# Key pages laid out with features on partitions, and weights laid out tile by tile, in a two-layer decoder step

## The chip, the cores and the metric

The kernel runs on one core of a Trainium2 chip. The metric is the device time of one execution in microseconds (us). Engines are named as the profile names them: PE (TensorE, matrix products; PEld its weight loads), DVE (VectorE), ACT (ScalarE), POOL (GpSimd), and SP (SyncE, which issues most DMAs here). A "q" behind an engine's name means its sequencer, as where it issues a DMA.

## The reference

One inference step of a decoder with two layers, for a prompt of 1024 tokens and for 8 sequences of 8 sample tokens, all in float32. Layer 0 is stick-breaking attention, layer 1 an RWKV-7 recurrence; each is followed by a squared-ReLU MLP, and each of the four sub-layers has a norm with shift, scale and gate made from a conditioning vector (adaLN). What matters here is the attention of the sample tokens: each sequence has 2048 past keys and values in 16 pages of 128 tokens, and a page table says where in the pool they lie.

```python
def sb_attend(q, k, v, q_pos, k_pos, bias):
    z = einsum('bqhd,bkhd->bhqk', q, k) * (SB_HEAD_DIM ** -0.5) + bias[None, :, None, None]
    mask = k_pos[None, :] < q_pos[:, None]
    log_beta = log_sigmoid(z)
    log_1mb = where(mask, log_beta - z, 0.0)
    tail = cumsum(log_1mb, axis=3, reverse=True) - log_1mb
    a = where(mask, exp(log_beta + tail), 0.0)
    return einsum('bhqk,bkhd->bqhd', a, v)

past_k = cache_k[layer][page_table]     # 8 sequences x 16 pages x 128 tokens x 16 heads x 64
past_v = cache_v[layer][page_table]
```

The weight of a key depends on all later keys, so a sequence is worked through from its last page to its first with a carried product.

## The kernel before

Activations lie with features on partitions, in 8 tiles of 128 features, and the tokens on the free axis in two halves: A (576 columns, the 64 sample tokens among them) and B (512). A dense layer (`dense`, L354) takes one tile of 128 outputs at a time. `weight` (L340) loads the tile's weights (wst; 128 x 8 x 128, or 128 x 4 x 128 for the MLP's second half) straight from the row-major matrix, so that each descriptor moves 128 floats, 512 bytes. ACT rounds them to wh, POOL and DVE make the rest wl, and PE sums three products for each tile of inputs (dq at L364 to L366).

Behind the dense layers runs other work, as a generator: after every so many dense products one step of it is put into the program (`step`, `behind`). `background` (L1588) holds the prompt's attention of both halves, then the attention of the samples (`att_sample`, L671), then the recurrence. While the samples are attended to, half A's MLP is the dense work, and its weights are asked for by ACT's queue rather than by SP's (`self.sampling`). The written order is only a start: the scheduler puts the instructions of each engine in order by its own estimates of time, and gives the DMAs of both queues the semaphores that they wait for.

`att_sample` takes two pages a step, 64 steps in all, 8 for a sequence:

- `page_id` (L663) reads two page numbers from the table into SP's registers.
- `page_k` (L652, DMA at L657) loads a key page as it lies, tokens first, in four DMAs of a quarter of the features each: 32 partitions (key modulo 32), in each 4 runs of 256 floats. Two page buffers (`KB`) are used in turn.
- `turned` (L701, L705) transposes the page on DVE, 32 x 32 blocks at a time, into kT; this is why the features of a page were cut into tiles of (feature / 256, feature % 32). Two buffers (`KTB`).
- `scores` (L708, L714): for each of the two pages 8 products of the queries (qbd, every head in its own columns, made by `queries`, L689) with 128 columns of kT, into zs.
- `stick` (L555): sigmoid on ACT, 1 - beta on POOL, a scan and a product on DVE.
- the weights are transposed on PE (tq), copied to aTs, and multiplied with the value pages into os (L771). `page_v` (L645, DMA at L648) loads a value page in one DMA of 128 partitions with 4 KB each; five buffers (`VB`) in turn.

The scores of the next step stand ahead of this step's products, and the pages for it are asked for before that. `new_keys` handles a sequence's 8 new tokens ahead of its first step.

The vectors of features (biases, gains and the like) are loaded in rows of 128 by many small DMAs and transposed on PE in three groups (`load_params`, L147), and the conditioning vectors likewise (`load_c`, L180). The adaLN weights are read by blocks of 256 columns, 1 KB a descriptor (`ada_steps`).

Of the kernel before, what the change touches and what calls it, by code (L numbers as in the profile page):

```python
# [31 lines left out]
KTB = 2  # L32
# [32 lines left out]
def make_consts():  # L65
# [20 lines left out]
    for h in range(16):  # L86
        c[p // 8 == 4 * (h % 4) + h // 4, C_H16 + h] = 1.0
# [6 lines left out]
class Kern:  # L94
# [19 lines left out]
    def copy(self, out, in_, eng=None):  # L114
        """PSUM or SBUF to SBUF, on ScalarE and VectorE in turn."""
        if eng is None:
            eng = "a" if self.flip() else "v"
        if eng == "a":
            self.nc.scalar.copy(out, in_)  # L119
        elif eng == "v":  # L120
            self.nc.vector.tensor_copy(out, in_)  # L121
        else:
            self.nc.gpsimd.tensor_copy(out, in_)
# [23 lines left out]
    def load_params(self, groups, tmp, ps, tag):  # L147
        """Vectors of features: rows of 128 on partitions, then features on partitions."""
        nc, I = self.nc, self.I
        for group in groups:  # L150
            nrow = sum(n for _, _, n in group)
            nat = tmp.tile([128, 128], F32, tag="n", name="pnat")
            r = 0
            for name, ap, n in group:
                flat = ap if len(ap.shape) == 1 else ap.rearrange("a b -> (a b)")
                nc.sync.dma_start(nat[r:r + n, :], flat.rearrange("(a b) -> a b", b=128))
                r += n
            q = ps.tile([128, 512], F32, tag=tag, name="pps")
            self.transpose(q[:, :nrow], nat[:nrow, :])
            par = self.misc.tile([128, nrow], F32, name="par_" + group[0][0])  # L160
            self.copy(par, q[:, :nrow])
            r = 0
            for name, ap, n in group:
                self.par[name] = par[:, r:r + n]
                r += n

    def params(self):
        I = self.I
        ada = lambda s: (f"b{s}", I["ada_b_" + ("mix", "ffn")[s % 2]][s // 2], 24)
        vec = lambda n: (n, I["rw_" + n][0], 8)  # L170
        self.par = {}
        return [
            [ada(0), ("norm_mix", I["norm_mix"], 16)],
            [ada(1), ada(2), ada(3), ("norm_ffn", I["norm_ffn"], 16), ("final", I["final_norm"], 8)],
            [("mu", I["rw_mu"][0], 48)] + [vec(n) for n in ("w0", "a0", "k_k", "k_a", "r_k", "ln_g",
                                                           "ln_b")],
        ]

# [1 line left out]
    def load_c(self, tmp, ps):  # L180
        nc, I = self.nc, self.I
        c = tmp.tile([72, 128], F32, tag="n", name="c")
        nc.sync.dma_start(c[0:8], I["c_prompt"].rearrange("v (k p) -> (v k) p", p=128))
        nc.sync.dma_start(c[8:72], I["c_sample"].rearrange("v (k p) -> (v k) p", p=128))
        s = tmp.tile([72, 128], F32, tag="n", name="cs")
        nc.scalar.activation(s, c, AF.Sigmoid)
        nc.vector.tensor_mul(s, s, c)
        q = ps.tile([128, 512], F32, tag="dps", name="cps")
        self.transpose(q[:, 0:72], s)
        self.cT = self.misc.tile([128, NT, 32], F32, name="cT")  # L190
        nc.vector.memset(self.cT, 0.0)
        nc.vector.tensor_copy(self.cT[:, :, 0:9], q[:, 0:72].rearrange("p (v k) -> p k v", v=9))
# [32 lines left out]
    def ada_steps(self, s, ps, tag, blocks=range(12)):  # L225
        """mod[:, j, v]: feature tile j of shift (0-7), scale (8-15), gate (16-23); vector v.
        The scale tiles end up as norm gain * (1 + scale)."""
        nc, I = self.nc, self.I
        i, kind = s // 2, ("mix", "ffn")[s % 2]
        w = I["ada_w_" + kind][i]  # L230
# [20 lines left out]
        for n in blocks:  # L251
            q = ps.tile([128, 512], F32, tag=tag, name="adaq")
            for u in range(0, NT, kt):
                st = pool.tile([128, kt, 256], F32, tag=stage, name="adaw")
                nc.sync.dma_start(st, w[u * 128:(u + kt) * 128, n * 256:(n + 1) * 256]
                                  .rearrange("(k p) c -> p k c", p=128))
# [15 lines left out]
    def rms(self, x, pt, tmp, ps, tag, slot, rslot=None):  # L272
        """1 / sqrt(mean square + eps) of every token, on all partitions: [128, W]."""
# [26 lines left out]
    def modulate(self, s, f, x, R, pt, t):  # L300
        """t = x * R * A of feature tile f, of samples with B added; returns B of the prompt."""
# [18 lines left out]
    def norm_split(self, s, x, R, pt, pool, tmp, slot):  # L320
        """Rounded parts of (x * R) * A + B."""
# [48 lines left out]
    def residual(self, s, x, pt, tmp):  # L370
        """evac of a dense layer: x += gate * out."""
# [17 lines left out]
    def load_x(self, pt, pool, ps, early):  # L389
        """Generator; the tiles are in self.x. early: all loads first."""  # L390
# [27 lines left out]
    def to_tokens(self, m, pt, t, dst_p, dst_s, tmp, ps):  # L418
        """Feature tile m of the columns of pt; rows of tokens to DRAM."""
# [19 lines left out]
    def qkv(self, hi, lo, pt, tmp, ps):  # L439
        I, O = self.I, self.O  # L440
        w = I["sb_w_qkv"][0]
# [4 lines left out]
        self.dense_to(w[:, D:2 * D], hi, lo, pt, tmp, ps, self.s_k0,  # L446
# [5 lines left out]
        self.dense_to(w[:, 2 * D:], hi, lo, pt, tmp, ps, None, value)  # L452

# [9 lines left out]
    def load_split(self, src, pt, pool, tmp, parts):  # L463
        """Generator: rounded parts of feature tiles in DRAM."""
# [19 lines left out]
    def ffn(self, s, x, hi, lo, pt, pool, tmp, ps):  # L484
        """x += gate * (relu(h @ w_up) ** 2) @ w_down, the hidden layer 512 at a time."""
# [3 lines left out]
        for b in range(8):  # L489
# [14 lines left out]
            self.dense(wd[512 * b:512 * b + 512], range(NT), [uh[k] for k in ks],  # L504
                       [ul[k] for k in ks], pt, ps, res)

# [1 line left out]
    def att_setup(self, lp):  # L508
# [7 lines left out]
        # of the two heads of a feature tile, 64 rows each  # L516
# [9 lines left out]
    def att_stacks(self, m, pt, sp):  # L526
        """Rounded parts of q and k of the two heads of tile m, the parts of k on top of each other."""
# [27 lines left out]
    def stick(self, z, w, bias, bp, tag, carry, mask):  # L555
        """z: scores in PSUM [128, w], keys in order; returns weights a and the product of 1 - beta."""
# [17 lines left out]
    def att_prompt(self, m, pt, sp, bp, ps):  # L574
        """Generator over the query tiles (128 of a head, or 64 of both) of the two heads of tile m."""
# [69 lines left out]
    def page_v(self, sp, r):  # L645
        t = sp.tile([128, D], F32, tag="pv", name="pagev", bufs=VB)
        src = self.I["cache_v"][0].rearrange("n p h d -> n p (h d)")
        ins = self.nc.sync.dma_start(t, src[bass.ds(r, 1)].rearrange("o p f -> (o p) f"))  # L648
# [3 lines left out]
    def page_k(self, sp, r):  # L652
        """[128 (feature / 256, key % 32), key / 32, feature % 256]"""
        t = sp.tile([128, D], F32, tag="pk", name="pagek", bufs=KB)
        src = self.I["cache_k"][0].rearrange("n (i k) h d -> n k i (h d)", i=4)
        for x, a in enumerate(self.R4):
            ins = self.nc.sync.dma_start(  # L657
                t[a].rearrange("k (i f) -> k i f", i=4),
# [1143 lines left out]
```

## Time and profile before

| | us |
|---|---|
| median of 3 runs | 4046.95 (4046.1, 4046.95, 4064.11) |
| span of the profiled execution | 4045.0 |
| PE busy | 3675.1 |
| DVE busy | 2499.4 |
| ACT busy | 1491.1 |
| POOL busy | 1322.8 |

For the profiled execution the profile has its span, from the first to the last instruction; no other time of it is known, and the two closest runs lie 1.1 and 1.95 us above that span. The profile's second part cuts the span into 40 slices of 101 us and gives busy shares in tenths. A stretch of any length can be asked for in the same way, and so can the waits in it, the DMAs that its queues issued, and each instruction. In a row of a wait stand who waited, for whom, the total in us, how many times, and the longest. A matmul in float32 is two instructions in the profile.

### The profile page before, as it was taken

Reading aid. Unit: us, or ns where it says so; the run is one execution under the profiler, and the core shown is the slowest. Engines: PE = TensorE matmul, PEld = TensorE weight load, DVE = VectorE, ACT = ScalarE, POOL = GpSimd, SP = SyncE. Lnnn points to the kernel's source line nnn. Section 1 sums busy time; section 2 is a strip of 40 time slices with the busy share of each in tenths; the row PEclk is TensorE's granted clock in tenths of the full one; section 3 lists DMA queues with packets and bytes.
Section 4 is the critical chain, followed back from the end, with each engine's and each line's share of the span. In section 5 each row is a group of like instructions: output and inputs, shape, how many; then the busy total and the mean of one; then the engine's idle time right before and its main releaser. Section 6 shows DMA issues by size and latency. Waiting matters only on the chain. (4 is left out here: it accounts for less than half of the span.)

```text
span 4045.0 us, 76587 instructions
## 1 busy us (share of the span) xinstructions
PE 3675.1 (91%) x27756; PEld 2899.0 (72%) x27756; DVE 2499.4 (62%) x4907; ACT 1491.1 (37%) x3132; POOL 1322.8 (33%) x1844
## 2 busy tenths in 40 slices
PE   8989999899887888799779999999889999998998
PEld 6776667677666666577657777665688888876887
DVE  4256777886555455668775555677884666645444
ACT  4123444543121122455333444554434333433332
POOL 1135555563111111222243333433222222233442
PEclk9999999999999999799789999898899999999999
DMA  9965434125999999856645444556735444342332
GB/s 283 292 186 164 153 114 102 49 67 140 236 236 215 216 228 231 239 169 217 180 118 139 127 129 131 173 179 212 215 110 138 116 121 137 96 133 76 102 98 78
DMA packets 873728, 641.63 MB, mean 159 GB/s; under 512 B 174195, under 2 KB 793004, under 8 KB 873350
## 3 DMA queue, kind: packets, MB, share of 16 engines
q1 hardware_dynamic: 804198, 602.12, 52.8%
q10 hardware_dynamic: 69152, 34.61, 3.9%
q8 instruction: 220, 3.60, 0.4%
q14 instruction: 158, 1.29, 0.1%
HBM read 521.62 MB, written 114.92 MB: 157 GB/s over the span
## 5 line engine op out<-in xcount | busy, mean ns | idle before, releaser
L350 POOL TENSOR_TENSOR wl<-wst,wh 128x256 fp32r<-128x256 f32 (+1 forms) x512 | 641.3, 1254 | 1553.0 <-ACT wh L348 1353.0
L364 PE MATMUL dq<-hhi,wh 128*128 128x288 f32 (+1 forms) x2112 | 717.9, 341 | 29.4 <-ACT hhi L119 22.5
L348 ACT CAST wh<-wst 128x512 fp32r<-128x512 f32 (+1 forms) x512 | 424.6, 834 | 825.7 <-PE dq L365 546.2
L365 PE MATMUL dq<-hlo,wh 128*128 128x288 f32 (+1 forms) x2112 | 713.6, 338 | 7.7 <-POOL hlo L318 4.7
L366 PE MATMUL dq<-hhi,wl 128*128 128x288 f32 (+1 forms) x2112 | 715.9, 339 | 0.0
L365 PE MATMUL dq<-ul,wh 128*128 128x288 f32 (+1 forms) x1536 | 514.8, 335 | 0.0
L351 DVE TENSOR_TENSOR wl<-wst,wh 128x256 fp32r<-128x256 f32 (+1 forms) x512 | 349.5, 685 | 267.1 <-ACT wh L348 251.1
L366 PE MATMUL dq<-uh,wl 128*128 128x288 f32 (+1 forms) x1536 | 512.9, 335 | 0.0
L364 PE MATMUL dq<-uh,wh 128*128 128x288 f32 (+1 forms) x1536 | 511.2, 337 | 1.4 <-DVE x L379 0.6
L364 PEld LDWEIGHTS dq<-hhi,wh 128*128 128x128 f32 x2112 | 407.3, 193 | 72.9 <-ACT hhi L119 23.2
L365 PEld LDWEIGHTS dq<-hlo,wh 128*128 128x128 f32 x2112 | 406.9, 193 | 54.2 <-issue 14.4
L366 PEld LDWEIGHTS dq<-hhi,wl 128*128 128x128 f32 x2112 | 407.0, 193 | 49.5 <-issue 18.7
L379 DVE SCALAR_TENSOR_TENSOR x<-dq,mod,x 128x288 f32<-128x288 f32 (+1 forms) x432 | 243.2, 565 | 207.5 <-PE dq L366 204.8
L364 PEld LDWEIGHTS dq<-uh,wh 128*128 128x128 f32 x1536 | 292.2, 191 | 42.4 <-issue 14.1
L705 DVE STREAM_TRANSPOSE kT<-pagek 128x1024 f32<-128x1024 f32 x128 | 159.0, 1243 | 255.3 <-DMA pagek<-cache_k 240.5
L366 PEld LDWEIGHTS dq<-uh,wl 128*128 128x128 f32 x1536 | 293.1, 191 | 31.1 <-issue 8.3
L365 PEld LDWEIGHTS dq<-ul,wh 128*128 128x128 f32 x1536 | 292.7, 191 | 30.2 <-issue 8.5
L570 DVE TENSOR_TENSOR_SCAN prod<-prod 128x256 f32<-128x256 f32 (+5 forms) x264 | 259.6, 986 | 87.5 <-POOL prod L564 48.5
L564 POOL TENSOR_SCALAR prod<-beta 128x256 f32<-128x256 f32 (+5 forms) x264 | 169.2, 642 | 270.9 <-ACT beta L561 238.4
L364 PE MATMUL dq<-xhi,wh 128*128 128x288 f32 (+1 forms) x576 | 210.0, 365 | 4.5 <-DVE dn L121 2.1
L365 PE MATMUL dq<-xlo,wh 128*128 128x288 f32 (+1 forms) x576 | 203.4, 353 | 7.2 <-DVE xlo L318 5.5
L714 PE MATMUL zs<-kT,qbd 128*32 128x128 f32 x2048 | 95.4, 301 | 123.0 <-DVE kT L705 118.3
(327 smaller groups left out, 6684.4 us busy)
## 6 DMA issues: line engine op xcount, KB each, us to landing
pagek<-cache_k SPq DMA_DIRECT2D x512, 128.0 KB
pagev<-cache_v SPq DMA_DIRECT2D x128, 512.0 KB
wst<-w_up SPq DMA_DIRECT2D x96, 512.0 KB
wst<-w_down SPq DMA_DIRECT2D x192, 256.0 KB
st<-s_st SPq DMA_DIRECT2D x40, 672.0 KB
wst<-sb_w_qkv SPq DMA_DIRECT2D x48, 512.0 KB
adaw<-ada_w_mix SPq DMA_DIRECT2D x96, 256.0 KB
adaw<-ada_w_ffn SPq DMA_DIRECT2D x96, 256.0 KB
```

Of the source, the lines that this page charges most:

```text
L348: nc.scalar.copy(wh, st)
L350: nc.gpsimd.tensor_sub(wl[:, :h], st[:, :h], wh[:, :h].bitcast(F32))
L351: nc.vector.tensor_sub(wl[:, h:], st[:, h:], wh[:, h:].bitcast(F32))
L364: nc.tensor.matmul(q, wh[:, k, :], h, start=k == 0, stop=False)
L365: nc.tensor.matmul(q, wh[:, k, :], l, start=False, stop=False)
L366: nc.tensor.matmul(q, wl[:, k, :], h, start=False, stop=k == kt - 1)
L379: nc.vector.scalar_tensor_tensor(xs, q[:, :np_], g, xs, ALU.mult, ALU.add)
L564: nc.gpsimd.tensor_scalar(p[:, :w], beta[:, :w], -1.0, 1.0, ALU.mult, ALU.add)
L570: nc.vector.tensor_tensor_scan(r, r, r, 1.0 if carry is None else carry, ALU.mult, ALU.bypass)
L705: nc.vector.transpose(kT[-1].rearrange("p i m k -> p (i m k)"), t)
L714: nc.tensor.matmul(z[32 * g:32 * g + 32, 128 * pg:128 * pg + 128], qbd[:, m, :], kT[:, :, m, :], start=p == 0, stop=p == 1)
```

## The change

Inputs are laid out anew on the host before the launch (`laid_out`). In the key cache, each page becomes 128 rows (the feature within a tile of 128) of 8 x 128 floats (tile, token). A key page is then one DMA like a value page, and the scores read it as it lies: `turned` and kT are gone. The two pages of a step share one buffer of 8 KB a partition (still `KB` = 2 of them, as many bytes as the two page buffers and two kT were), and one product of 256 columns covers both pages. Features are in tiles of 128 everywhere now, so queries, new keys and outputs of the samples are sorted in plain tiles, with fewer and wider loads and stores.

Every weight is laid out tile by tile, so that a partition's part of a tile is one run of 4 KB (2 KB for `w_down` and for the adaLN blocks of two tiles). The small matrices of the low-rank products are laid out likewise. All vectors of features come as one array with features on partitions, in one DMA; the conditioning vectors as another. No arithmetic is done on the host.

```diff
     def weight(self, ap):
-        kt = ap.shape[0] // 128
+        kt = ap.shape[1]
         st = self.wp.tile([128, kt, 128], F32, tag="wst", name="wst")
         q = nc.scalar if self.sampling else nc.sync
-        q.dma_start(st, ap.rearrange("(k p) c -> p k c", p=128))
+        q.dma_start(st, ap)
...
-            wh, wl = self.weight(w[:, m * 128:(m + 1) * 128])
+            wh, wl = self.weight(w[m])
...
-    def page_k(self, sp, r):
-        t = sp.tile([128, D], F32, tag="pk", name="pagek", bufs=KB)
-        src = self.I["cache_k"][0].rearrange("n (i k) h d -> n k i (h d)", i=4)
-        for x, a in enumerate(self.R4):
-            ins = self.nc.sync.dma_start(
-                t[a].rearrange("k (i f) -> k i f", i=4),
-                src[bass.ds(r, 1), :, :, 256 * x:256 * x + 256].rearrange("o k i f -> (o k) i f"))
+    def page_k(self, t, r):
+        ins = self.nc.sync.dma_start(
+            t.rearrange("p m k -> p (m k)"),
+            self.I["cache_kT"][bass.ds(r, 1)].rearrange("o p f -> (o p) f"))
         self.paged.append(ins)
-        return t
...
         def keys(b, j):
             rs = [self.page_id(b, 2 * j + pg) for pg in range(2)]
-            return [self.page_k(sp, r) for r in rs], rs
-
-        def turned(kp):
-            kT = []
-            for t in kp:
-                kT.append(bp.tile([128, 4, NT, 32], F32, tag="kT", name="kT", bufs=KTB))
-                nc.vector.transpose(kT[-1].rearrange("p i m k -> p (i m k)"), t)
-            return kT
+            t = sp.tile([128, 2, NT, 128], F32, tag="pk", name="pagek", bufs=KB)
+            for pg, r in enumerate(rs):
+                self.page_k(t[:, pg], r)
+            return t, rs
 
-        def scores(qbd, kTs):
+        def scores(qbd, kp):
             z = ps.tile([128, 512], F32, tag="z", name="zs")
-            for pg, kT in enumerate(kTs):
-                for p in range(2):
-                    for g in range(4):
-                        m = 2 * g + p
-                        nc.tensor.matmul(z[32 * g:32 * g + 32, 128 * pg:128 * pg + 128],
-                                         qbd[:, m, :], kT[:, :, m, :], start=p == 0, stop=p == 1)
-                yield z
+            for p in range(2):
+                for g in range(4):
+                    nc.tensor.matmul(z[32 * g:32 * g + 32, :256].rearrange("p (i k) -> p i k", i=2),
+                                     qbd[:, 2 * g + p, :], kp[:, :, 2 * g + p, :], start=p == 0,
+                                     stop=p == 1)
+            return z
...
+    a["cache_kT"] = kc.reshape(n, 128, NT, 128).transpose(0, 3, 2, 1).reshape(n, 128, D)
+    a["params"] = np.concatenate([v.reshape(-1, 128) for v in vectors]).T
+    a["ada_w"] = np.stack([tiles(w, 256) for w in ada])
+    a["w_up"] = np.stack([tiles(w) for w in f["w_up"]])
```

How the order moves, at two places. First SP's queue in the middle of the samples' attention, before the change: a step's two key pages (pagek, four DMAs each, one of them shown), its value pages (pagev), and the reading of page numbers from the table (pt).

```order
L657 DMA pagek_12527<-cache_k 32x4x256
L657 ISA
...
L657 DMA pagek_12532<-cache_k 32x4x256
...
L648 DMA pagev_12652<-cache_v 128x1024
L648 ISA
L648 DMA pagev_12654<-cache_v 128x1024
L668 TENSOR_LOAD pt_512
L668 ISA x2
```

The same queue with the change; a pair of key pages is one buffer with one name, and has two DMAs (one of them shown).

```order
L620 DMA pagev_11228<-cache_v 128x1024
...
L627 DMA pagek_11248<-cache_kT 128x1024
...
L620 DMA pagev_11358<-cache_v 128x1024
L637 TENSOR_LOAD pt_480
...
L620 DMA pagev_11360<-cache_v 128x1024
...
L627 DMA pagek_11380<-cache_kT 128x1024
...
L620 DMA pagev_11485<-cache_v 128x1024
```

Ten page DMAs a step become four, and the numbers are now read between the two value pages. Value page 11360 takes the buffer of the fifth value page before it, 11097, and the pair 11380 is asked for right behind it.

Second, PE at the same place, the dense products between these rows left out. Before the change, one step: scores of the two pages (zs), the transposes of the weights (tq), products with the values (os).

```order
L714 MATMUL zs_12716<-kT_12684,qbd_11905 32x128 x8
L127 MATMUL tq_12765<-cst_60,beta_12688 128x128 x2
...
L714 MATMUL zs_12716<-kT_12686,qbd_11905 32x128 x8
...
L771 MATMUL os_12068<-pagev_12652,aTs_12768 32x256 x4
L771 MATMUL os_12068<-pagev_12654,aTs_12768 32x256 x4
```

With the change, three steps in a row.

```order
L674 MATMUL zs_11141<-pagek_11119,qbd_10421 32x256 x8
...
L731 MATMUL os_10571<-pagev_11097,aTs_11182 32x256 x4
L731 MATMUL os_10571<-pagev_11099,aTs_11182 32x256 x4
...
L674 MATMUL zs_11269<-pagek_11248,qbd_10421 32x256 x8
...
L731 MATMUL os_10571<-pagev_11226,aTs_11316 32x256 x4
L731 MATMUL os_10571<-pagev_11228,aTs_11316 32x256 x4
...
L674 MATMUL zs_11399<-pagek_11380,qbd_10421 32x256 x8
...
L731 MATMUL os_10571<-pagev_11358,aTs_11443 32x256 x4
L731 MATMUL os_10571<-pagev_11360,aTs_11443 32x256 x4
```

The scores of both pages are one group of 8 now, with one wait. The pair 11380 can be asked for when the product with page 11097 (first group) is through, and its scores stand in the third group. Elsewhere each kind of work stands at nearly the same place among the dense products as before, with small moves of single products.

More of the change, by code (lines that the diff above doesn't have):

```diff
@@ L180, in load_c, with load_params @@
[L180 to L185, printed above, removed]
+    def load_params(self):
+        n = sum(n for _, n in PARAMS)
+        par = self.misc.tile([128, n], F32, name="par")
+        self.nc.sync.dma_start(par, self.I["params"])
+        self.par, r = {}, 0
+        for name, n in PARAMS:
+            self.par[name] = par[:, r:r + n]
+            r += n
@@ L503, in ffn @@
             self.dense(wu, ks, hi, lo, pt, ps, evac)
-            self.dense(wd[512 * b:512 * b + 512], range(NT), [uh[k] for k in ks],
+            self.dense(wd[b], range(NT), [uh[k] for k in ks],
                        [ul[k] for k in ks], pt, ps, res)
@@ L668, in page_id @@
             return self.nc.sync.value_load(self.pt[0:1, n:n + 1], min_val=0,
-                                           max_val=self.I["cache_k"].shape[1] - 1)
+                                           max_val=self.I["cache_kT"].shape[0] - 1)
     def att_sample(self, sp, bp, ps):
@@ L743, in att_sample @@
         kp, rs = keys(*steps[0])
-        for z in scores(qbd, turned(kp)):
-            yield
+        z = scores(qbd, kp)
+        yield
         o = carry = None
         for n, (b, j) in enumerate(steps):
-            V = [self.page_v(sp, r).rearrange("p (x g d) -> p x g d", x=4, g=4) for r in rs]
+            V = [self.page_v(sp, r) for r in rs]
             if n + 1 < len(steps):
@@ L760, in att_sample @@
                     qbd = queries(b + 1)
-                for z in scores(qbd, kT):
-                    yield
+                z = scores(qbd, kp)
+                yield
+                yield
             tq = ps.tile([128, 512], F32, tag="t", name="tq")
@@ L1776, in psum @@
         return PS
-IN = ["x_prompt", "x_sample", "cache_k", "cache_v", "state_wkv", "state_shift", "page_table",
-      "c_prompt", "c_sample", "norm_mix", "ada_w_mix", "ada_b_mix", "norm_ffn", "ada_w_ffn",
-      "ada_b_ffn", "w_up", "w_down", "sb_w_qkv", "sb_w_o", "sb_bias", "rw_mu", "rw_w_r", "rw_w_k",
-      "rw_w_v", "rw_w_o", "rw_w0", "rw_w1", "rw_w2", "rw_a0", "rw_a1", "rw_a2", "rw_g1", "rw_g2",
-      "rw_k_k", "rw_k_a", "rw_r_k", "rw_ln_g", "rw_ln_b", "final_norm"]
+AS_IS = ["x_prompt", "x_sample", "state_wkv", "state_shift", "page_table",
+         "sb_bias"]
@@ new lines, with laid_out, tiles @@
+PARAMS = [("b0", 24), ("b1", 24), ("b2", 24), ("b3", 24), ("norm_mix", 16), ("norm_ffn", 16),
+          ("final", 8), ("mu", 48)] + [(n, 8) for n in ("w0", "a0", "k_k", "k_a", "r_k", "ln_g", "ln_b")]
+def laid_out(inputs):
+    f = {n: np.asarray(a) for n, a in inputs.items()}
+    def tiles(w, c=128):
+        K, M = w.shape
+        return w.reshape(K // 128, 128, M // c, c).transpose(2, 1, 0, 3)
+    ada = [f["ada_w_" + ("mix", "ffn")[s % 2]][s // 2] for s in range(4)]
+    vectors = [f["ada_b_" + ("mix", "ffn")[s % 2]][s // 2] for s in range(4)]
+    vectors += [f["norm_mix"], f["norm_ffn"], f["final_norm"], f["rw_mu"]]
+    vectors += [f["rw_" + n] for n, _ in PARAMS[8:]]
+    c = np.concatenate([f["c_prompt"], f["c_sample"]])
+    wa2 = np.concatenate([f["rw_w2"][0], f["rw_a2"][0]])
+    a = {n: f[n] for n in AS_IS}
+    kc, vc = f["cache_k"][0], f["cache_v"][0]
+    n = len(kc)
+    a["cache_v"] = vc.reshape(n, 128, D)
+    a["cache_kT"] = kc.reshape(n, 128, NT, 128).transpose(0, 3, 2, 1).reshape(n, 128, D)
+    a["c"] = c.reshape(9, NT, 128).transpose(2, 1, 0)
+    a["params"] = np.concatenate([v.reshape(-1, 128) for v in vectors]).T
+    a["ada_w"] = np.stack([tiles(w, 256) for w in ada])
+    a["w_up"] = np.stack([tiles(w) for w in f["w_up"]])
+    a["w_down"] = np.stack([[tiles(w[512 * b:512 * b + 512]) for b in range(8)] for w in f["w_down"]])
+    for n in ("sb_w_qkv", "sb_w_o", "rw_w_r", "rw_w_k", "rw_w_v", "rw_w_o"):
+        a[n] = tiles(f[n][0])
+    a["rw_wa1"] = tiles(np.concatenate([f["rw_w1"][0], f["rw_a1"][0]], 1))[0]
+    g1 = f["rw_g1"][0].reshape(NT, 128, 160).transpose(1, 0, 2)
+    a["rw_g1a"], a["rw_g1b"] = g1[:, :, :128], g1[:, :, 128:]
+    a["rw_wa2"] = wa2.reshape(128, NT, 128).transpose(1, 0, 2)
+    a["rw_g2"] = f["rw_g2"][0].reshape(160, NT, 128).transpose(1, 0, 2)
+    a["consts"] = make_consts()
+    return {n: np.ascontiguousarray(x) for n, x in a.items()}
```

128 lines of the change are left out of this document (44 added, 84 removed).

## The prediction

> **What bounds the kernel now.** I read the page's first two parts, then stages, then waits, then the DMA of the one stage that the change touches most.
>
> ```profile
> span 4045.0 us, 76587 instructions
> PE 3675.1 (91%) x27756; PEld 2899.0 (72%) x27756; DVE 2499.4 (62%) x4907; ACT 1491.1 (37%) x3132; POOL 1322.8 (33%) x1844
> ...
> PE   8989999899887888799779999999889999998998
> ...
> DMA  9965434125999999856645444556735444342332
> ```
>
> TensorE is busy 91% of the span, so time is lost where its row shows 7 and 8. The longest such place is slices 11 to 16, and there the DMA row reads 9: this is the attention of the samples, which reads 128 key pages and 128 value pages. The stages, cut finer (columns: stretch, length, busy time and instructions of each engine, granted clock, DMA share, GB/s):
>
> ```profile
> core 0: us, PE busy (x) PEld busy (x) DVE busy (x) ACT busy (x) POOL busy (x), PEclk, DMA share, GB/s
> 975.00:1650.00 675.00, 545.25 (x5626) 439.56 (x5624) 359.85 (x616) 143.02 (x290) 122.50 (x253) 0.93 0.96 231
> 1011.00:1600.00 589.00, 477.82 (x4917) 387.14 (x4909) 309.99 (x525) 119.50 (x251) 106.03 (x224) 0.93 0.95 226
> 400.00:600.00 200.00, 192.62 (x1199) 131.83 (x1199) 142.25 (x204) 80.46 (x163) 101.79 (x180) 0.97 0.43 128
> 707.00:809.00 102.00, 90.67 (x671) 65.67 (x670) 90.37 (x119) 51.07 (x97) 57.03 (x83) 0.93 0.17 51
> ```
>
> 975 to 1650 us is the stage; 1011 to 1600 us is its steady part, on which I do the sums. There TensorE idles 589 - 478 = 111 us, DMA is at 0.95, and VectorE has half its time free. Who waits for whom in the steady part (total us, times, longest):
>
> ```profile
> DVE kT L705 <- DMA pagek<-cache_k: 199.9, 82, 6.5
> PE zs L714 <- DVE kT L705: 96.1, 66, 4.6
> ```
>
> 96 of the 111 idle us are one wait: the scores (zs) wait for a transposed key page (kT), which waits for the page's landing. So key pages landing late bound this stage. What moves there:
>
> ```profile
> DMA packets 120024, 133.40 MB, mean 226 GB/s; under 512 B 9461, under 2 KB 106484, under 8 KB 119956
> pagek<-cache_k SPq DMA_DIRECT2D x421, 128.0 KB
> pagev<-cache_v SPq DMA_DIRECT2D x104, 512.0 KB
> wst<-w_down ACTq DMA_DIRECT2D x45, 256.0 KB
> wst<-w_up ACTq DMA_DIRECT2D x20, 512.0 KB
> ```
>
> In MB of a million bytes: keys 421 x 128 KB = 55.2, values 104 x 512 KB = 54.5, weights 22.3. And how fast each goes when it is alone. Two stretches of 2 us that hold value pages (194 packets for 0.71 MB in the first), two of key pages (480 for 0.44 MB in the second), then one of 1 KB rows on all 128 partitions (the adaLN weights, early on):
>
> ```profile
> 1040.00:1042.00 2.00, 1.37 (x9) 1.14 (x9) 0.47 (x1) 0.10 (x1) 0.00 (x0) 1.00 0.98 355
> 1466.00:1468.00 2.00, 0.47 (x8) 0.00 (x0) 1.17 (x1) 0.00 (x0) 0.00 (x0) 1.00 1.01 378
> 1093.00:1095.00 2.00, 2.00 (x17) 2.00 (x17) 0.00 (x0) 0.46 (x2) 0.00 (x0) 1.00 1.14 222
> 1152.00:1154.00 2.00, 2.00 (x11) 2.00 (x10) 0.36 (x1) 0.17 (x1) 0.00 (x0) 0.50 1.12 220
> 30.00:35.00 5.00, 5.00 (x43) 2.88 (x43) 2.28 (x9) 0.56 (x2) 0.00 (x0) 1.00 1.10 349
> ...
> DMA packets 194, 0.71 MB, mean 355 GB/s; under 512 B 17, under 2 KB 22, under 8 KB 194
> ...
> DMA packets 480, 0.44 MB, mean 220 GB/s; under 512 B 51, under 2 KB 480, under 8 KB 480
> ```
>
> With the engines full in both, values go at 355 to 378 GB/s and keys at 220. The fifth row says that 1 KB packets alone are not the reason (349). What sets the key loads apart is their shape: a quarter page each, on 32 partitions.
>
> **The change part by part.** *Key pages.* They take the value pages' form, 512 KB on 128 partitions in 4 KB rows, so I give them the value pages' rate. The steady part's 133.4 MB then need 133.4 / 0.355 = 376 us of DMA (at the 328 to 349 GB/s of slower rows about 400). That is under TensorE's work, so TensorE becomes the bound.
>
> *Scores.* 16 products of 128 columns a step become 8 of 256, the form that the value products (os) have now:
>
> ```profile
> L705 DVE STREAM_TRANSPOSE kT<-pagek 128x1024 f32<-128x1024 f32 x105 | 130.5, 1243 | 214.3 <-DMA pagek<-cache_k 199.9 <-PE os L771 8.0 <-PE dq L366 2.2
> L714 PE MATMUL zs<-kT,qbd 128*32 128x128 f32 x1692 | 77.4, 297 | 98.0 <-DVE kT L705 96.1 <-DVE beta L571 1.7
> L771 PE MATMUL os<-pagev,aTs 128*32 128x256 f32 x848 | 61.7, 402 | 0.8 <-DVE aTs L121 0.8
> ```
>
> 848 instructions are 53 steps of 16; the scores will also be 16 a step, so 77.4 becomes 61.7: TensorE's work falls from 478 to 462 us. The 105 transposes (130.5 us of VectorE) go, but VectorE is busy 310 of 589 us, so they only matter as a link (1.2 us and two hand-overs) between landing and scores.
>
> *Clock.* The granted clock is 0.93, since long waits are followed by slow products:
>
> ```profile
> 1419.04 1.08 PE L714 MATMUL zs<-kT,qbd 128*32 128x128 f32 x16 [4.55 <-DVE kT L705]
> ...
> 1421.34 0.44 PE L364 MATMUL dq<-hhi,wh 128*128 128x288 f32 x1
> 1421.58 0.44 PE L365 MATMUL dq<-hlo,wh 128*128 128x288 f32 x1
> ...
> 1425.10 0.30 PE L365 MATMUL dq<-hlo,wh 128*128 128x288 f32 x1
> 1425.24 0.29 PE L366 MATMUL dq<-hhi,wl 128*128 128x288 f32 x1
> ```
>
> After a wait of 4.55 us dense products start every 0.24 us, and only some 5 us later every 0.14. If those waits go, up to 0.07 x 589 = 41 us of work go with them; part of the slow time is idle anyway, so between 0 and 41 I take the middle, about 22: 462 becomes 440 (ends 462 and 421). [...]
>
> *What idle time stays.* The prompt's attention runs the same chain (scores, sigmoid, scan, transposes, products) with DMA at 0.43, and TensorE is busy 192.62 / 200 = 96% there (row 400 to 600). 440 / 0.963 = 457 us for the steady part, 132 less than 589. The whole stage is 675 / 589 = 1.146 times that: **151 us** less. The 25 us behind it (1650 to 1675) are not counted:
>
> ```profile
> 1650.00:1675.00 25.00, 13.24 (x104) 8.57 (x104) 23.93 (x26) 16.40 (x26) 13.99 (x16) 0.52 0.98 288
> ```
>
> VectorE is busy 23.9 of 25 us there with the next layer's norm, which the change leaves.
>
> *Wait added.* The scores now wait for two pages in one buffer, and behind them in TensorE's order stand value and dense products, which every other engine follows. SP's order and TensorE's (shown with the change) have a pair of pages requested two score groups before its use, some 17 us, for 3 us of transfer. SP itself, which takes most of a step for eight key DMAs, has room:
>
> ```profile
> 1203.36 7.89 SPq L657 DMA_DIRECT2D pagek<-cache_k  x8
> 1211.49 1.53 SPq L648 DMA_DIRECT2D pagev<-cache_v  x2
> ```
>
> Four issues in the value pages' form are some 3 us of an 8.6 us step.
>
> *Weights in tiles.* 512 B packets become 2 and 4 KB. Where weights were alone in this stage, the engines took 81.9% of 2 us for 0.48 MB:
>
> ```profile
> q10 hardware_dynamic: 953, 0.48, 81.9%
> ```
>
> That is 0.48 / 1.64 = 290 GB/s; at 355 the 22.3 MB take 63 us instead of 77, already in the 376. Outside this stage TensorE hardly waits for a load (its largest such wait is 7.0 us in all):
>
> ```profile
> PE gq L1031 <- DMA gb<-rw_g: 7.0, 4, 3.7
> ```
>
> Between nothing and some 15 us (twice this row) I take 5. *Vectors of features* come laid out: three transposes and some fifteen small DMAs go. At the start the 8 MB of adaLN weights set the pace (349 GB/s above), so only the end shows:
>
> ```profile
> 46.04 0.41 PE L127 MATMUL pps<-cst,pnat 104*128 104x104 f32 x1 [1.90 <-DMA pnat<-rw_ln_b]
> 46.14 0.59 PE L364 MATMUL dq<-hhi,wh 128*128 128x288 f32 x1
> ```
>
> The first dense product stands behind that wait: 2 us. The new-key products, queries and the sorting of outputs keep their numbers and sizes to within a few small copies, on POOL and VectorE, which have half their time free: nothing.
>
> *Sum.* 151 + 5 + 2 = 158 us, from the execution's 4045.0 us of span; the median of the runs, 4046.95 us, is 2 us above it. 4047 - 158 = **3889 us**. Ends: without idle time and with the full clock 421 us, 168 x 1.146 + 7 = 200 less, 3847; the other end is the first rival.
>
> **The rivals.** *A new wait takes part of the gain.* DMA (376 to 400 us) and TensorE (440) come close, so pages may still land late now and then, with the clock not recovering. TensorE is then busy as in the row of 707 to 809 us, 90.67 / 102 = 89%, with work of 462: 520 us, 79 + 7 less: **3961**. For it: the old kernel needs 589 us for 55.2 / 0.22 + 54.5 / 0.355 + 77 = 481 us of transfers, 1.22 times; 376 x 1.22 = 459, as much as TensorE's own. Against it: two steps of lead.
>
> *Key pages don't get faster.* If their rate came from where the pages lie in DRAM, it would stay, and with it the 589 us: 4047 - 7 = **4040**. Against it: values lie in pages scattered by the same table and go at 355. [...]
>
> *Slower.* Were a pair of pages requested only when the products of the step before are through, the 4 pages (2.1 MB / 0.355 = 5.9 us) would lie open in each of 64 steps: 8.6 + 5.9 = 14.5 us a step against 589 / 53 = 11.1 now, 64 x 3.4 = 217 us more, **4257** after the 7 elsewhere. It decides from 2.5 us of open transfer a step. For it: one buffer now holds two pages, and is free only when TensorE has read both. Against it: the order.
>
> **How the numbers follow.** Forecast 0.74, new wait 0.17, no faster keys 0.05, slower 0.04. The forecast's own range is 3847 to 3915 (the upper end with the clock left at 0.93: 462 / 0.963 = 480, 125 + 7 less); with the first rival the range is 3847 to 3965, which leaves out the other two. About 0.5% (20 us) is what can be told from no change: faster 0.91, same 0.05, slower 0.04.
>
> **What would show it.** Right: key pages at 340 GB/s or more while alone; the stage 520 to 530 us instead of 675; zs waiting for DMA under 20 us in all; granted clock 0.97 or more there; other stages within a few us. Wrong: zs <- DMA pagek at 60 us or more (first rival), DMA share still 0.95 with 220 GB/s for keys (second), a wait of several us in every step (third), or a loss elsewhere, where the scheduler laid out the rest anew.

## The result, and the profile after

| | before | with the change |
|---|---|---|
| median, us | 4049.95 (4 runs, 4046.1 to 4064.11) | 3866.54 (4 runs, 3863.52 to 3873.36) |
| ratio | | 0.9548, 95% interval 0.9529 to 0.9568 |
| span of the profiled execution, us | 4045.0 | 3864.6 |
| first to last score product (zs), us | 975.8 to 1690.8 | 972.3 to 1482.8 |

The change is 4.5% faster, 180 us by the spans. The first two parts of the page of the changed kernel, the same rows as were shown of before:

```profile
span 3864.6 us, 72940 instructions
PE 3630.1 (94%) x26728; PEld 2847.0 (74%) x26728; DVE 2360.7 (61%) x4777; ACT 1499.5 (39%) x3128; POOL 1342.7 (35%) x1844
...
PE   8998999999999998987799999898899999979998
...
DMA  8865543312888985567345445567444344433332
```

(A slice is 97 us now.) The samples' attention fills slices 11 to 15 and the first part of 16, where it reached from 11 into 17; TensorE's row has 9s there instead of 7s and 8s, and the DMA row four 8s and one 9 instead of 9s. The same stage by stretches (columns as in the prediction), with its middle first, then all of it but the two ends:

```profile
1000.00:1400.00 400.00, 400.00 (x3869) 322.51 (x3868) 202.69 (x402) 113.16 (x235) 119.92 (x217) 1.00 0.87 322
966.00:1449.00 483.00, 483.00 (x4640) 392.12 (x4639) 244.74 (x487) 139.32 (x284) 145.76 (x257) 1.00 0.88 323
```

TensorE has no idle time in 483 us, its granted clock is 1.00 (before: 0.93), and the DMA engines have room. The costliest wait of the kernel before, the scores' for a key page, is all but gone; the waits over the whole stage (960 to 1490 us) have only these two left, of the products and of their weight loads:

```profile
PEld zs L674 <- DMA pagek<-cache_kT: 1.9, 1, 1.9
PE zs L674 <- DMA pagek<-cache_kT: 1.0, 1, 1.0
```

Before, it was 96.1 us behind the transposes alone, in 589 us. The products of the two kinds, in the 400 us of the middle (counted in instructions, two to a product, as in the prediction):

```profile
L674 PE MATMUL zs<-pagek,qbd 128*32 128x256 f32 x816 | 57.2, 385 | 0.0
L731 PE MATMUL os<-pagev,aTs 128*32 128x256 f32 x816 | 54.8, 384 | 0.0
```

816 are 51 steps of 16, so **a step takes 400 / 51 = 7.84 us**; before, it took 589 / 53 = 11.11.

For "where", one more count is used below: the dense products (dq, 13824 in either kernel) are numbered in the order in which they start in the trace, and the times are set side by side. From product 2830 (the stage's start) to 5240 (its end) the kernel before takes 711.7 us and the changed one 520.6: 191 us less. The rest of the program gives 11 of them back.

### The profile page after: what moved, and what is told of

Read it like the earlier page. It is cut to its first block, busy times and chain, and to the rows that moved or that the text cites. A ratio compares the mean times of both kernels' runs of the same rounds, so it can differ in the third digit from the quotient of the medians.

```text
span 3864.6 us, 72940 instructions
## 1 busy us (share of the span) xinstructions
PE 3630.1 (94%) x26728; PEld 2847.0 (74%) x26728; DVE 2360.7 (61%) x4777; ACT 1499.5 (39%) x3128; POOL 1342.7 (35%) x1844
## 4 chain that ended last, share of the span: by engine, by line
PE 44%; DVE 6%; DMA 5%; issue 2%; SPq 2%; POOL 1%; ACT 1%; DVEq 0%; ACTq 0%; POOLq 0%
PE dq L337 12%; PE dq L338 12%; PE dq L339 11%; PE qc L1318 1%; DVE tm L1198 1%; DVE lxn L1200 1%; PE qc L1308 1%; PE qc L1327 1%; DMA st<-s_st 1%; DMA t<-s_y 1%; SPq L1205 1%; PE yq L1498 1%; PE s L1135 0%; PE selq L1423 0%; PE qc L1331 0%
## 5 line engine op out<-in xcount | busy, mean ns | idle before, releaser
L323 POOL TENSOR_TENSOR wl<-wst,wh 128x256 fp32r<-128x256 f32 (+1 forms) x512 | 653.3, 1277 | 1510.6 <-ACT wh L321 1297.7
L339 PE MATMUL dq<-hhi,wl 128*128 128x288 f32 (+1 forms) x2112 | 705.3, 334 | 1.0 <-POOL wl L323 1.0
L324 DVE TENSOR_TENSOR wl<-wst,wh 128x256 fp32r<-128x256 f32 (+1 forms) x512 | 376.3, 737 | 269.4 <-ACT wh L321 245.4
L339 PE MATMUL dq<-xhi,wl 128*128 128x288 f32 (+1 forms) x576 | 200.8, 349 | 0.0
L471 DVE TENSOR_TENSOR ut<-ut 128x288 f32<-128x288 f32 (+1 forms) x192 | 153.1, 798 | 42.9 <-ACT ut L470 39.8
```

Of the source, the lines that this page charges most:

```text
L323: nc.gpsimd.tensor_sub(wl[:, :h], st[:, :h], wh[:, :h].bitcast(F32))
L324: nc.vector.tensor_sub(wl[:, h:], st[:, h:], wh[:, h:].bitcast(F32))
L339: nc.tensor.matmul(q, wl[:, k, :], h, start=False, stop=k == kt - 1)
L471: nc.vector.tensor_mul(t[:, :n], t[:, :n], t[:, :n])
```

## The experiments

All steps below are counted as above, from 1000 to 1400 us: 400 us over the scores' matmul instructions that start there (16 a step, 32 where products have 128 columns). The kernel before has 11.19 us by this count. Its median beside the runs lay between 4044.57 and 4054.65.

| | us | ratio (95%) | us a step | DMA share, GB/s |
|---|---|---|---|---|
| change | 3866.54 | 0.9548 (0.9529 to 0.9568) | 7.84 | 0.87, 322 |
| e1 keys alone | 3895.57 | 0.9609 (0.9579 to 0.9639) | 7.84 | 0.92, 323 |
| e2 weights and vectors alone | 4032.83 | 0.9951 (0.9936 to 0.9967) | 10.67 | 0.94, 239 |
| e3 transposes kept | 3917.01 | 0.9664 (0.9634 to 0.9694) | 8.51 | 0.82, 295 |
| e4 four DMAs, 32 partitions | 4001.61 | 0.9901 (0.9873 to 0.9929) | 10.06 | 0.94, 251 |
| e5 four DMAs, 1 KB runs | 3960.7 | 0.98 (0.9772 to 0.9828) | 9.70 | 0.79, 258 |
| e6 one pair buffer | 3866.74 | 0.9554 (0.9527 to 0.9582) | 8.33 | 0.86, 307 |
| e7 one DMA, 1 KB runs | 3865.85 | 0.9551 (0.9529 to 0.9572) | 7.84 | 0.92, 321 |
| e8 two DMAs, 64 partitions | 4004.71 | 0.9888 (0.9871 to 0.9904) | 10.53 | 0.94, 242 |
| e9 three DMAs, 64 in the middle | 3927.39 | 0.9696 (0.968 to 0.9712) | 8.89 | 0.95, 280 |
| e10 other rate of the chains | 3863.66 | 0.9545 (0.9529 to 0.9561) | 7.84 | 0.87, 322 |
| e11 weights in 512 B packets | 3885.81 | 0.9588 (0.9571 to 0.9606) | 7.84 | 0.90, 313 |

### Which part does it: e1, e2, e3

e1 is the kernel before with the key cache's new layout, and all that follows from it, but with the old weights and vectors of features.

> The kernel before with the key pages of the change alone (page layout, one DMA a page, scores straight from it); weights, vectors and conditioning stay row-major. If landing key pages bounded the stage: first to last score product near 515 us (715 before, 510 with the whole change), granted clock 1.00 there, 3865 to 3890 us in all. If the smaller packets of the weights took a good part of the DMA's time: stage 560 us or more, 3920 or more.

e2 is the reverse: weights and vectors as in the change, and the key pages as before.

> The change without its key pages: weights tile by tile, vectors and conditioning laid out, key pages as before with four quarter DMAs and VectorE transposes. If key pages bounded the stage: stage 690 to 715 us, 4025 to 4048 us in all (the prediction's 7 us and a little less DMA). If the weights' packets took a good part of the DMA's time: 4000 or less, stage 660 or less.

Measured: 3895.57 and 4032.83. The keys alone bring 154 of the 183 us between the medians and the same step of 7.84 us; weights and vectors bring about 20 alone (0.5%), and 29 on top of the keys. The keys carry the gain, though e1 lies a little above the stated window (3865 to 3890). e2's time is in its window, but its stage is not: from the first to the last score product it takes 680 us (973.5 to 1653.7), less than the 690 expected at least, and the rest of the program gives part of that back.

e3 keeps the transposes on VectorE, but lets them work on pages that come as whole pages do in the change. Its pages lie in DRAM so that the transposed 32 x 32 blocks come out right:

```diff
+        def turned(kp):
+            kT = []
+            for t in kp:
+                kT.append(bp.tile([128, NT, 128], F32, tag="kT", name="kT", bufs=2))
+                nc.vector.transpose(kT[-1].rearrange("p m k -> p (m k)"),
+                                    t.rearrange("p m k -> p (m k)"))
+            return kT
...
-    a["cache_kT"] = kc.reshape(n, 128, NT, 128).transpose(0, 3, 2, 1).reshape(n, 128, D)
+    kT = kc.reshape(n, 128, NT, 128).transpose(0, 3, 2, 1).reshape(n, 4, 32, 32, 32)
+    a["cache_kT"] = kT.transpose(0, 1, 4, 3, 2).reshape(n, 128, D)
```

> The change with the transposes put back: pages are stored so that each lands in one DMA of 128 partitions with 4 KB rows, in two page buffers, and VectorE's transpose by 32 x 32 blocks into two kT buffers gives the form that the scores read, 16 products of 128 columns a step. If the landing rate was the bound: most of the gain stays, stage 520 to 560 us, 3880 to 3920 us in all, TensorE waiting for kT under 40 us. If the transposes as a link between landing and scores were what cost the time: 3960 or more, and TensorE still waits for kT by 80 us or more.

Measured: 3917.01, in the window for a bound by landing. The groups of e3 from 1000 to 1400 us:

```profile
L675 DVE STREAM_TRANSPOSE kT<-pagek 128x1024 f32<-128x1024 f32 x93 | 115.1, 1238 | 52.7 <-DMA pagek<-cache_kT 52.4 <-PE dq L339 0.2
L685 PE MATMUL zs<-kT,qbd 128*32 128x128 f32 x1504 | 67.8, 279 | 3.5 <-DVE kT L675 3.3
```

The transposes take as long as before (1238 ns), and the products have 128 columns as before; yet the scores' wait for them is 3.3 us, where the kernel before has 66.5 in the same 400 us. From e2, which has the same weights, to the change a step gets 2.83 us shorter: 2.16 of it come with the landing (10.67 to 8.51), and 0.67 with the transposes and narrow products going (8.51 to 7.84; 50 us in the medians).

### What made the old key pages slow: e4, e5, e7, e8, e9

All five are the change with the key page brought in another way; what TensorE computes stays. e4 splits the page's DMA by partitions, in four of 32:

```diff
-        ins = self.nc.sync.dma_start(
-            t.rearrange("p m k -> p (m k)"),
-            self.I["cache_kT"][bass.ds(r, 1)].rearrange("o p f -> (o p) f"))
+        for x in self.R4:
+            ins = self.nc.sync.dma_start(
+                t[x].rearrange("p m k -> p (m k)"),
+                self.I["cache_kT"][bass.ds(r, 1), x].rearrange("o p f -> (o p) f"))
```

> The change, but each key page comes in four DMAs of 32 partitions with 4 KB rows (before: 32 partitions, 1 KB runs). If the 32 partitions made key loads slow: 200 to 240 GB/s while keys are alone, scores wait for pages by 50 us or more in all, 3930 to 4040 us. If the 1 KB runs did: 340 GB/s or more, 3860 to 3885.

e5 splits it by columns instead, in four of 128 partitions with 1 KB each:

```diff
+        for x in range(4):
+            ins = self.nc.sync.dma_start(
+                t[:, 2 * x:2 * x + 2].rearrange("p m k -> p (m k)"),
+                self.I["cache_kT"][bass.ds(r, 1), :, 256 * x:256 * x + 256]
+                .rearrange("o p f -> (o p) f"))
```

> The change, but each key page comes in four DMAs of 128 partitions with 1 KB runs. If the 32 partitions made key loads slow: 340 GB/s or more while keys are alone, 3860 to 3885 us. If the 1 KB runs did: 200 to 240 GB/s, scores wait for pages, 3930 or more.

Measured: e4 4001.61, e5 3960.7. e4 gives back 135 us although its runs are 4 KB long, as the theory of 32 partitions says. Over its stage (970 to 1615 us) the scores wait 73 us, 32.8 of them put down to key pages and 27.3 to value pages. Its stretch from 1000 to 1400 us:

```profile
1000.00:1400.00 400.00, 341.27 (x3062) 269.39 (x3058) 160.72 (x320) 87.85 (x184) 93.16 (x174) 0.94 0.94 251
```

e5 misses the window of the theory of 32 partitions by far and lies where the theory of small packets had it, but its stage doesn't look like slow transfers. First its stretch from 1000 to 1400 us, then its score products there:

```profile
1000.00:1400.00 400.00, 400.00 (x3086) 273.25 (x3084) 161.51 (x323) 90.75 (x186) 94.11 (x176) 1.00 0.79 258
```

```profile
L676 PE MATMUL zs<-pagek,qbd 128*32 128x256 f32 x660 | 115.7, 389 | 0.0
```

The DMA engines are *less* busy than in the change (0.79), TensorE's row of products shows no wait, and yet it gets through 3086 instructions instead of 3869. "Busy 400 of 400" doesn't mean as much work: a score instruction takes 115.7 / 660 = 0.175 us of its time where the change has 57.2 / 816 = 0.070. The timeline of e5 shows why (times, engine, line, instruction; x2 is one product, two instructions):

```profile
1206.03 0.62 PE L676 MATMUL zs<-pagek,qbd 128*32 128x256 f32 x2
...
1206.58 0.33 PE L126 MATMUL tq<-cst,beta 128*128 128x128 f32 x1
...
1206.84 0.62 PE L676 MATMUL zs<-pagek,qbd 128*32 128x256 f32 x2
...
1207.39 0.33 PE L126 MATMUL tq<-cst,beta 128*128 128x128 f32 x1
...
1207.78 0.62 PE L676 MATMUL zs<-pagek,qbd 128*32 128x256 f32 x2
...
1208.33 0.19 PEld L338 LDWEIGHTS dq<-hlo,wh 128*128 128x128 f32 x1 [0.41 <-issue]
...
1208.79 1.05 PE L676 MATMUL zs<-pagek,qbd 128*32 128x256 f32 x10
...
1209.77 0.40 PE L337 MATMUL dq<-hhi,wh 128*128 128x288 f32 x1
```

A product needs one tile of features, and so one quarter only: the first four products of a step read the four quarters in turn. The scheduler put them in one by one, with other products between them, 4.2 groups of scores a step instead of 1.1. One product by itself takes 0.55 us until the next kind starts; five in a row take 0.98. Counted over the 400 us, the score groups cost 2.44 us a step instead of 1.02, and the dense groups, cut more often too, 5.86 instead of 5.50: 1.78 of the 1.86 us that a step is longer than in the change. The weight loads (PEld) show a pause at these places: in the row above, the first load of 128 columns of weights behind the scores' 32 (128\*32) stands after 0.41 us of idle time put down to "issue". Over the 400 us the gaps put down to "issue" come to 95 us in 298 places, against 53 us in 177 in the change. Why the engine pauses there is not shown. So e5 mixed two things, and e7 takes them apart: one DMA a page again, but with 1 KB runs.

```diff
-            t.rearrange("p m k -> p (m k)"),
-            self.I["cache_kT"][bass.ds(r, 1)].rearrange("o p f -> (o p) f"))
+            t.rearrange("p (q m) k -> p q (m k)", q=4),
+            self.I["cache_kT"][bass.ds(r, 1)].rearrange("o q p f -> (o p) q f"))
...
+    a["cache_kT"] = a["cache_kT"].reshape(n, 128, 4, 256).transpose(0, 2, 1, 3)
```

> Only the layout of a key page in DRAM differs from the change: the page is still one DMA on 128 partitions, but a partition's 4 KB come as four runs of 1 KB. This parts the two things that e5 mixed. Theory (packet size is not what made the keys slow; e5 lost its time because the score products, which need one quarter of the features each, were cut into four small groups a step between dense products, 4.2 groups where the change has 1.1): here one product needs the whole page again, so the groups stay whole and the time is within 15 us of the change's 3867, 3855 to 3885, with the stage at 8.0 to 8.2 us a step. Rival (1 KB runs are slow by themselves): as e5, 3930 or more, with DMA busy above 0.95 in the stage.

Measured: 3865.85, the change's own time, with 7.84 us a step (a little below the 8.0 expected at least) and 1.1 groups:

```profile
1000.00:1400.00 400.00, 397.89 (x3843) 321.21 (x3842) 201.41 (x399) 112.55 (x234) 119.67 (x216) 1.00 0.92 321
```

Packets of 1 KB were not what made the keys slow. They do keep the DMA engines busier, 0.92 instead of 0.87 for the same rate, but there was room.

e8 and e9 ask which property of 32 partitions it was, by the loop of e4 over other slices. In e8 they are partitions 0 to 63 and 64 to 127:

```diff
-        for x in self.R4:
+        for x in self.R2:
```

> A key page in two DMAs of 64 partitions, 0 to 63 and 64 to 127, 4 KB runs. [...] Theory B (the rate grows with the number of partitions): 64 partitions lie halfway between 220 and 355, 288 GB/s; a step's transfers are then 1.05/0.288 + 1.03/0.355 + 0.42/0.355 = 7.7 us against 8.8 at 220, and by e4's 10.06/8.8 = 1.14 some 8.8 us a step: 3890 to 3940.

And in e9, against e4 too:

```diff
-        for x in self.R4:
+        for x in (slice(32, 96), slice(0, 32), slice(96, 128)):
```

> A key page in three DMAs: partitions 32 to 95, 0 to 31, 96 to 127. [...] Theory B (number of partitions): half at 288 and half at 220, 249 GB/s: 9.5 us a step, 3950 to 3980, and slower than e8.

Measured: e8 4004.71, e9 3927.39. By theory B, the number of partitions, e8 was to be the faster of the two, at 3890 to 3940, and e9 at 3950 to 3980; both miss, and the sign is the other one: halves of 64 are as slow as quarters of 32 (10.53 us a step against 10.06), and the page cut in *three*, with 32 to 95 as one piece, is 77 us faster than the page cut in two. Stretches from 1000 to 1400 us of e8 and then of e9:

```profile
1000.00:1400.00 400.00, 331.66 (x2894) 262.37 (x2897) 149.40 (x298) 83.21 (x174) 88.46 (x162) 0.92 0.94 242
```

```profile
1000.00:1400.00 400.00, 362.17 (x3361) 288.39 (x3360) 176.34 (x348) 96.97 (x206) 102.37 (x192) 0.97 0.95 280
```

Both have the DMA engines full (0.94, 0.95), at 242 and 280 GB/s; the scores' wait for key pages over the stage is 90.7 us in e8 and 31.4 in e9. A cost for each DMA, or SP's time to issue them, can't be the reason: e8 has half as many key DMAs as e4 and is as slow, and e9 has more than e8 and is faster. So it matters which partitions one DMA covers, and not their number alone. What sets 32 to 95 apart from 0 to 63 is not shown.

### The slower rival: e6

The change with one buffer for pairs of key pages instead of two (`KB = 1`), so that no pair can be asked for until the scores of the pair before are through.

> The change with one buffer for a pair of key pages instead of two (KB = 1), so that a pair can be asked for only when the scores of the pair before are through. This is the mechanism of the rival on the slower side, forced. If a step's dense work (about 5 us of the 8) covers a pair's 3 us of transfer and its landing: 3865 to 3920 us. If the lead of two score groups is what keeps the transfer hidden: 3 us or more open in each of 64 steps, 4060 or more.

Measured: 3866.74, no different from the change. SP's queue does wait for the scores now, from 1000 to 1400 us:

```profile
SPq L627 <- PE zs L674: 91.7, 43, 3.7
```

But TensorE's wait for the page over the stage (966 to 1449 us) stays at nothing:

```profile
PE zs L674 <- DMA pagek<-cache_kT: 3.5, 5, 1.8
```

The request goes out when the *scores* of a pair are through, not the step's other products; 5.5 us of dense products a step (counted in the change) come before the next ones, and hide a transfer of some 3 us (an estimate: a pair's 1.05 MB at the 355 GB/s of the prediction's row). (The longer step in the table is dense work that the scheduler moved into the stage, 2070 dense products in these 400 us instead of 1973: the total is the same.)

### Where weights gain, and where gain was lost: e10, e11

In the changed kernel TensorE waits before one of the last layers' projections; its timeline, ACT and PE:

```profile
3409.22 0.46 ACT L1501 ACTIVATE yT<-yq,par 128x128 f32<-128x128 f32 x1 [6.06 <-PE yq L1498]
...
3420.51 0.62 ACT L118 CAST shi<-t 128x512 fp32r<-128x512 f32 x1 [9.72 <-DMA t<-s_y]
...
3421.18 1.65 PE L337 MATMUL dq<-shi,wh 128*128 128x512 f32 x3 [6.13 <-ACT shi L118]
```

The projection reads the recurrence's output back from DRAM (s_y), and its last tile was only just made (yT). From dense product 12000 to 12287 the kernel takes 79.0 us, the one before 62.0. e10 tries to let the recurrence end earlier, at rate 4 behind the dense products:

```diff
-            self.rate = RC
+            self.rate = RC + i
```

> In the change the last output projection waits 7.8 us for shi, the recurrence's output, and its clock falls; there 16 us of the gain are lost between dense products 12100 and 12200. Here the chains of the second half run at rate 4 instead of 3 behind the dense products, so they end earlier. Theory (the recurrence ends too late there): the wait goes, 3845 to 3860. Rival (what is taken forward there costs as much elsewhere, or the scheduler sets the place whatever the rate): 3860 to 3885.

Measured: 3863.66, not told from the change, and not a test of the theory: with either rate the recurrence's products stand at the same places among the dense products (3804 of them before dense product 11500), so the rate as written is not what sets the order. That the late recurrence costs the 17 us is read from the trace, not shown by a run; what would bring it forward was not found.

e11 undoes only the layout of the dense weights, so that their DMAs move 512 bytes a packet again:

```diff
-        q.dma_start(st, ap)
+        q.dma_start(st, ap.rearrange("k p c -> p k c"))
...
+    def rows(w):
+        K, M = w.shape
+        return w.reshape(K // 128, 128, M // 128, 128).transpose(2, 0, 1, 3)
...
-    a["w_up"] = np.stack([tiles(w) for w in f["w_up"]])
+    a["w_up"] = np.stack([rows(w) for w in f["w_up"]])
...
-        a[n] = tiles(f[n][0])
+        a[n] = rows(f[n][0])
```

> The change, but the matrices of the dense layers lie in DRAM as one block of 128 rows of 512 bytes for each tile of inputs, so that their DMAs go in packets of 512 bytes as before; adaLN weights, vectors of features and small matrices stay as in the change. The keys alone (e1) were 29 us above the change. Theory (the packets of the dense weights are that gap): 3885 to 3900. Rival (their landing is hidden behind dense products, 5 us at most, and the gap comes from the rest and from where the scheduler puts the work): 3862 to 3878.

Measured: 3885.81, 19 us above the change by the medians and 16 by the ratios; with the intervals of both ratios it is between some 6 and 27 us. The recurrence's products stand where they do in the change at each place compared, so the stretches can be set side by side: products 2700 to 2830 take 3.8 us more, 3000 to 5183 8.3, 5240 to 6000 6.7, together 18.8, and the others add up to 0.6. Nearly all of it lies in the samples' attention, just ahead of it, and in the 200 us behind it. ACT waits longer for the MLP's weights; over the whole execution, e11 and then the change:

```profile
ACT wh L321 <- DMA wst<-w_up: 26.0, 8, 6.6
```

```profile
ACT wh L321 <- DMA wst<-w_up: 3.3, 2, 2.7
```

In e11 19.0 of the 26.0 us lie between 940 and 1650 us, where the change has none. TensorE itself has no wait for a weight there. In the three stretches its idle time is 9 us longer than in the change, behind ACT's and VectorE's work for the attention and the next layer's norm, and the rest goes with a lower clock (0.93 instead of 1.00 in the first, 0.92 instead of 0.96 in the last). That the late weights delay that work on ACT fits these rows, but no run shows it.

The other 10 us between e11 and e1 (adaLN weights, vectors, small matrices, and a different order) are not settled.

## Why the prediction was right, and which terms were mis-sized

It said 3889, in 3847 to 3965; the time is 3866.54. By its steps:

- **What bounds the stage** held, and the stage went further than the sign given for it: the dense products that took from 975 to 1650 us take 489 us now, not 520 to 530. e3, which takes away only the slow landing, has three quarters (2.16 of 2.83 us) of what the keys bring to a step.
- **Key pages at the value pages' rate** held. The prediction's test was 340 GB/s or more while keys are alone; a key page's packets look like a value page's now, so the test is made on both: in the 200 stretches of 2 us between 1000 and 1400 us, 109 have the DMA engines at 0.97 or more, and their median is 396 GB/s (before: 126 stretches, 228; e7 377, e9 284, e4 246, e8 243). That is also more than the 355 assumed; two of the fastest:

```profile
1342.00:1344.00 2.00, 2.00 (x23) 1.57 (x16) 1.68 (x4) 0.62 (x1) 1.02 (x4) 1.00 1.07 421
1378.00:1380.00 2.00, 2.00 (x25) 1.26 (x25) 0.69 (x1) 0.26 (x1) 1.66 (x1) 1.00 1.03 420
```

- **Scores** held: 61.7 / 53 = 1.16 us a step predicted, 57.2 / 51 = 1.12 measured.
- **Clock and idle time** are the terms that were mis-sized. The prediction took half of the clock's 41 us and 3.7% of idle time, 457 / 53 = 8.6 us a step. The measured step of 7.84 is its low end (421 / 53 = 7.94): the clock came back whole, and no idle time stayed. The idle share was read from the prompt's attention, where the chain of scores, sigmoid and scan is the same; why that stage idles and this one doesn't was not tested. From 966 to 1449 us TensorE has no wait at all, and its granted clock is 1.00. Over 64 steps the difference is (8.6 - 7.84) x 64 = 49 us. In the steady part of the kernel before (1011 to 1600 us) the trace has the clock at half 19 times, 78.5 us in all; that is some 39 us of lost work, the 41 of the sum. Only two of the 19 go with a wait of TensorE about as long as the 4.55 us of the prediction's row (that one itself, and 4.48), the others with waits of 1.4 to 3.3 us. Here is one of them, the product behind the wait and then the stretch behind it with its clock, and below it the same of the change, at the end of its stage:

```profile
1349.81 1.06 PE L714 MATMUL zs<-kT,qbd 128*32 128x128 f32 x16 [2.29 <-DVE kT L705]
```

```profile
1350.00:1353.00 3.00, 3.00 (x25) 2.62 (x18) 1.89 (x9) 0.95 (x3) 1.10 (x4) 0.50 1.06 277
```

```profile
1485.72 0.41 PE L126 MATMUL tq<-cst,beta 128*128 128x128 f32 x2 [2.03 <-DVE beta L544]
```

```profile
1488.00:1491.00 3.00, 3.00 (x13) 2.76 (x12) 0.94 (x2) 0.54 (x2) 0.00 (x0) 0.52 0.22 55
```

So the full 41 us came back where the waits went altogether; by these rows, with 2.29 and 2.03 us ahead of a clock of 0.50 and 0.52, waits of 2 to 3 us that stayed would have kept part of the loss, as an estimate.
- **The stage's length** was taken as 1.146 times 53 steps, 60.7; there are 64 up to the last scores at 1690.8. At 2.5 us a step that is 8 us more. With 151 and 49 this makes 208; by the scores the stage is 204.5 us shorter (715.0 to 510.5). The 13 us between that and the 191 of the dense products come from the stage's ends, mostly the last: product 5240 started 4 us ahead of the last scores and starts 14 us behind them now.
- **Weights in tiles** were given 5 us, at most some 15; e11 has 16 to 19 for the dense weights alone, with an interval that takes in 15. The weak step was to count the weights of this stage in the DMA's 376 us and then let TensorE's work cover them: the whole share of the engines' time was there, but by the traces 12 us were lost in the stage and just ahead of it, and 7 behind it. That single weights came late is the likely reason, not a shown one.
- **The start** was given 2 us and has none. The first dense product starts at 33.6 instead of 46.1 us, but product 200 at 80.8 instead of 80.6: something else sets the pace there, the adaLN weights as the prediction has it, though no run tried that.
- **"Other stages within a few us"** is wrong piece by piece and nearly right in sum. Products 6600 to 6912 take 23.5 us more than before and 12000 to 12287 take 17.0 more, others less; in all 11 us of the stage's 191 are lost again. In the first of these stretches the scheduler put more of the recurrence (560 of its products come before dense product 6912, not 310, so the moves were not all as small as the section on the change says), which is work brought forward, and 6912 to 8640 take 13.5 us less. The second is the wait of e10.

Summed up: 191 us in the stage less 11 behind it and 1 ahead of it leaves 179 up to the last dense product, and the spans differ by 180; 158 were predicted. That the total is only some 22 us off is in part luck: the stage gained 40 us more than its 151, and the rest, given 7 us of gain, lost 12.

**The rivals.** A new wait of the scores for pages is not there (2.9 us in all, 60 were asked for). That keys would stay slow by where they lie falls with e4 and e8: the same pages, in the same places, are slow or fast by the partitions that one DMA covers. The slower rival needed 2.5 us of open transfer a step, and even e6 has 3.5 in the whole stage; it was wrong in what a request waits for.

## What to carry to other kernels

Ask of each large load not only how long its runs are, but which partitions *one* DMA covers: here a page on all 128 cost no time at 1 KB runs, pages in four pieces of 32 or in the halves 0 to 63 and 64 to 127 cost some 135 us, and pages with 32 to 95 as one piece 61. When all the waits go that a lower clock follows, count the whole of the clock's loss and not half (here 0.93 became 1.00), and read the share of engines that stay as a bound on throughput only: single transfers can still be late, as e11 suggests (ACT's wait of 26.0 us for w_up, against 3.3). Where the order is made by a scheduler, splitting a load also splits the work that reads it, and what any stage gains may come back in part where the order is laid anew.

## What was not expected of the hardware

- Reading both caches, one core moved a median of 396 GB/s, and 421 at most, in the stretches of 2 us with all DMA engines busy; 355 to 378 were the rows on which the prediction rested.
- In e5 TensorE's products show 100% busy, a clock of 1.00 and no wait, and are still 20% fewer than in the change (3086 instructions against 3869 in 400 us), with products of 32 columns of weights and of 128 one by one in turn; the row of the weight loads shows the pauses (95 us of "issue" against 53).
- In 589 us of the kernel before, the clock fell to half 17 times where no single wait of TensorE was longer than 3.3 us; the prediction's row has 4.55.
